# Attention scores of a head pair in a hybrid encoder kernel: zero-padded queries over all 128 rows against two heads on 64 rows each

## The chip, the cores and the metric

The kernel runs on one core of a Trainium2 chip. The metric is device time in microseconds (us) for one execution, as the median of several runs. The engines are named as in the profile: PE is the matrix engine and PEld its weight loads, DVE the vector engine, ACT the scalar engine, POOL the third elementwise engine, SP the queue that starts most transfers. A matmul here is two instructions: a load of the stationary operand (LDWEIGHTS, counted under PEld) and the MATMUL that streams the moving operand through it into PSUM. PSUM has eight banks of 128 partitions by 512 fp32 values.

## What is computed

The reference is an encoder of four layers on 512 tokens of width 1024: a convolution mixer, a neighbourhood attention, a retention, a convolution mixer, each followed by a gated feed-forward network. The change lies in the attention of layer 1 alone (16 heads of width 64, tokens on a grid of 8 rows by 64 columns):

```python
def nat_mixer(h, w_qkv, q_g, k_g, rpb, w_out):
    qkv = (h @ w_qkv).reshape(b, s, 3, NAT_HEADS, NAT_HEAD_DIM)
    q = rmsnorm(qkv[:, :, 0], q_g) * (NAT_HEAD_DIM ** -0.5)
    k = rmsnorm(qkv[:, :, 1], k_g)
    v = qkv[:, :, 2]
    ...
        sc = jnp.einsum('bhqd,bhrqwd->bhqrw', q_r, k_win).astype(jnp.float32)
        sc = sc + bias.transpose(0, 2, 1, 3)[None].astype(jnp.float32)
        p = jax.nn.softmax(sc.reshape(b, NAT_HEADS, GRID_W, kh * NAT_KW), axis=-1)
        ...
        return jnp.einsum('bhqrw,bhrqwd->bhqd', p, v_win)
    ...
    return out @ w_out
```

The scores `sc` are a product over the 64 values of one head.

## The kernel before

**Number format.** Every product is computed from fp32 data cut into a high and a low part of type fp32r; `mm3` (L158 to L161) issues three matmuls, high by high, high by low and low by high, into one PSUM region. `mm3s` (L164 to L166) is the same with the operands exchanged.

**The attention stage** (`nat`, L559) works on four groups `g` of four heads. `NORDER` says in which order its steps are written: `p0 a0 p1 a1 p2 w0 a2 p3 a3 w12 w3`. A step `p` (`proj`) projects q, k and v of a group: long runs of matmuls with 256 moving columns (L164 to L166). A step `a` (`att`) is the attention of a group, a step `w` (`wout`) the output projection of one or two groups, matmuls with 512 columns (L159 to L161, tiles oh and ol). The tile framework schedules the written program over the engines: it may move an instruction of one step between those of another, as its tiles and banks come free. So projections and attention stand mixed on PE, and each engine then executes its own list in order.

**Inside a step `a`** there are two pairs of heads (`pi` 0 and 1). `att_prep` (L635) transposes q and k of a pair on PE (L642), so that partitions 0 to 63 hold head 0 and 64 to 127 head 1, and copies them out of PSUM: k whole into kh and kl (L645, L646), q in four pieces into two tiles `qz[0]` and `qz[1]` (L650 on ACT, L651 on DVE). `qz[i]` has the queries of head `i` on that head's 64 partitions and zeros on the other 64; the zeros are written once at the head of the stage (L568 to L575, four DVE copies). `att_step` (L676) then handles one head and one half `pr` of the queries: it takes a PSUM bank S, writes the scores of two query blocks of 128 into it by `mm3`, with `qz[i]` as the stationary operand over all 128 rows of the array and 256 columns of kh or kl as the moving one (L683). The other head's keys meet the zeros. The softmax follows on DVE and ACT (L690 to L701), four transposes on PE (L703), the split into ph and pl (L706) and the product with v (L714: 12 matmuls with 64 stationary columns and 128 moving columns, shown as 128\*64). `att_pair` (L656) calls `att_step` for both heads, for each `pr`.

In all there are 4 groups, 2 pairs, 2 halves, 2 heads, 2 blocks and 3 products: 192 score matmuls.

Of the kernel before, what the change touches and what calls it, by code (L numbers as in the profile page):

```python
# [8 lines left out]
F32 = mybir.dt.float32  # L9
F32R = mybir.dt.float32r  # L10
I32 = mybir.dt.int32
AF = mybir.ActivationFunctionType
ALU = mybir.AluOpType
AX = mybir.AxisListType
MUL, ADD, SUB = ALU.mult, ALU.add, ALU.subtract
PSUM = bass.MemoryType.PSUM

P = 128
T = 512
# [51 lines left out]
def tile_trunk(  # L71
# [17 lines left out]
    def nm(s):  # L89
        uid[0] += 1  # L90
        return f"{s}{uid[0]}"
# [11 lines left out]
    def bank(which):  # L103
        return cur[which].tile([P, T], F32, tag="ps", name=nm("ps"))
# [25 lines left out]
    def pc(name, i=0, w=1):  # L130
        c = COLS[name] + i
        if c < 64:
            return png[:, c:c + w]
        return pt[:, c:c + w]
# [424 lines left out]
    def nat(after):  # L559
        PER = 4  # L560
        with ExitStack() as st:
# [3 lines left out]
            mask = np1.tile([P, 3, 256], F32, tag="mask", name=nm("mask"))  # L565
            nc.scalar.dma_start(mask, nmask.rearrange("p (v k) -> p v k", v=3))
            kstart = (0, 64, 192, 256)
            qzs = [[np1.tile([P, 2, T], F32R, tag=f"qz{n}{i}", name=nm("qz")) for i in range(2)]  # L568
                   for n in range(NQZ)]
            zz = np1.tile([P, 1], F32, tag="zz", name=nm("zz"))  # L570
            nc.vector.memset(zz, 0.0)
            for qz in qzs:
                for i in range(2):
                    zp = slice(64 - 64 * i, 128 - 64 * i)
                    nc.vector.tensor_copy(qz[i][zp], zz[zp].unsqueeze(2).broadcast_to([64, 2, T]))  # L575

            def part_proj(g, part):
                pss = [bank(psa), bank(psa)]
# [54 lines left out]
                return qk, va, vs  # L633

            def att_prep(g, pi, qk):  # L635
                qz = qzs[(2 * g + pi) % NQZ]
                kh = np2.tile([P, T], F32R, tag="kh", name=nm("kh"))
                kl = np2.tile([P, T], F32R, tag="kl", name=nm("kl"))
                for part in range(2):
                    ps = bank(psb)  # L640
                    for tb in range(4):
                        nc.tensor.transpose(ps[:, tb * P:(tb + 1) * P],  # L642
                                            qk[:, part, tb, pi * P:(pi + 1) * P], ident)
                    if part == 1:
                        nc.scalar.activation(kh, ps, AF.Copy, scale=pc("kg"))  # L645
                        nc.vector.scalar_tensor_tensor(kl, ps, pc("kg"), kh.bitcast(F32), MUL, SUB)  # L646
                    else:
                        for i in range(2):
                            r = slice(64 * i, 64 * i + 64)
                            nc.scalar.activation(qz[i][r, 0, :], ps[r], AF.Copy, scale=pc("qg")[r])  # L650
                            nc.vector.scalar_tensor_tensor(  # L651
                                qz[i][r, 1, :], ps[r], pc("qg")[r], qz[i][r, 0, :].bitcast(F32),
                                MUL, SUB)
                return qz, kh, kl

            def att_pair(g, pi, qz, kh, kl, va, vs):  # L656
                hi = np1.tile([P, T], F32R, tag="oh", name=nm("oh"), bufs=NO)
                lo = np1.tile([P, T], F32R, tag="ol", name=nm("ol"), bufs=NO)
                bms = []
                for i2 in range(2):  # L660
                    W = np2.tile([P, 384], F32, tag="W", name=nm("W"))
                    nc.sync.dma_start(W, wd[g * PER + pi * 2 + i2])
                    bm = np1.tile([P, 3, 256], F32, tag="bm", name=nm("bm"), bufs=NBM)
                    for vi, ws in enumerate((128, 64, 0)):
                        nc.gpsimd.tensor_tensor(bm[:, vi, :], W[:, ws:ws + 256],
                                                mask[:, vi, :], ADD)
                    bms.append(bm)
                for pr in range(2):
                    for i2 in range(2):
                        r = slice(64 * i2, 64 * i2 + 64)  # L670
                        c = slice(pr * 256, pr * 256 + 256)
                        op = att_step(g, pi, i2, pr, qz, kh, kl, bms[i2], va, vs)
                        state["att"] = split(op, hi[r, c], lo[r, c])
                return hi, lo

            def att_step(g, pi, i2, pr, qz, kh, kl, bm, va, vs):  # L676
                hh = pi * 2 + i2
                S = bank(psb)
                for i in range(2):
                    b = pr * 2 + i  # L680
                    ks = slice(kstart[b], kstart[b] + 256)
                    qs = slice(b * P, (b + 1) * P)
                    mm3(S[:, i * 256:(i + 1) * 256], qz[i2][:, 0, qs], qz[i2][:, 1, qs],  # L683
                        kh[:, ks], kl[:, ks], True, True)
                e = np1.tile([P, T], F32, tag="e", name=nm("e"), bufs=NE)
                mn, sx, rx = sm(2), sm(2), sm(2)
                for i in range(2):
                    vi = (0, 1, 1, 2)[pr * 2 + i]
                    ei = e[:, i * 256:(i + 1) * 256]
                    nc.vector.tensor_tensor_reduce(  # L690
                        ei, S[:, i * 256:(i + 1) * 256], bm[:, vi, :], -1.0, 3.0e38,
                        ADD, ALU.min, mn[:, i:i + 1])
                    nc.scalar.activation(ei, ei, AF.Exp, bias=mn[:, i:i + 1], scale=-1.0,
                                         accum_out=sx[:, i:i + 1])
                nc.vector.reciprocal(rx, sx)
                for i in range(2):
                    ei = e[:, i * 256:(i + 1) * 256]
                    if g == 3 and i == 1:
                        nc.scalar.activation(ei, ei, AF.Copy, scale=rx[:, i:i + 1])
                    else:  # L700
                        nc.vector.tensor_scalar(ei, ei, rx[:, i:i + 1], None, MUL)  # L701
                for i in range(4):
                    nc.tensor.transpose(S[:, i * P:(i + 1) * P], e[:, i * P:(i + 1) * P], ident)  # L703
                ph = np2.tile([P, T], F32R, tag="ph", name=nm("ph"))
                pl = np2.tile([P, T], F32R, tag="pl", name=nm("pl"))
                split(S, ph, pl)  # L706
                for i in range(2):
                    b = pr * 2 + i
                    vt, v0 = ((va, 0), (vs, 0), (vs, 1), (va, 2))[b]
                    oo = S[:64, i * P:(i + 1) * P]  # L710
                    for c in range(2):
                        hsl = slice(hh * HD, (hh + 1) * HD)
                        psl = slice((i * 2 + c) * P, (i * 2 + c + 1) * P)
                        mm3(oo, vt[:, v0 + c, 0, hsl], vt[:, v0 + c, 1, hsl],  # L714
                            ph[:, psl], pl[:, psl], c == 0, c == 1)
                return S[:64, :256]
# [472 lines left out]
```

## Time and profile before

| | us |
|---|---|
| median of 3 runs | 2584.52 (2584.17 to 2585.12) |
| profiled execution, whole | 2585.3 |
| its span, first to last instruction | 2583.5 |
| PE busy in the span | 2573.7 |
| attention stage, about | 584 to 836 of the span |

The span is what the profile's rows cover; the 1.8 us that the whole execution has beyond it lie outside. The stretches named below are in us from the span's start. A MATMUL's shown length includes the way through the array, so neighbours overlap; how fast matmuls follow each other is read from their starts. The granted clock of PE is 1.00 in every stretch shown, the higher of its two levels.

### The profile page before, as it was taken

How to read it: one execution, taken by the hardware profiler on the slowest of the kernel's cores; microseconds unless marked ns; L12 is line 12 of the kernel's file. 1: busy time of each engine (PE TensorE's matmuls, PEld its weight loads, DVE VectorE, ACT ScalarE, POOL GpSimd, SP SyncE). 2: the span in 40 equal slices, each digit the busy share in tenths (PEclk: the TensorE clock that was granted, in tenths of full speed). 3: DMA queues.
4: the chain of work that ended last, by engine and by line, in shares of the span. 5: the costliest groups of instructions: out<-in, count | busy, mean ns of one | idle time of the engine just before them, and what ended most of it. 6: DMA issues, size and time to landing. Idle time of an engine off the chain costs nothing.

```text
span 2583.5 us, 32274 instructions
## 1 busy us (share of the span) xinstructions
PE 2573.7 (100%) x12742; PEld 2138.2 (83%) x12742; DVE 1657.4 (64%) x2671; ACT 1047.0 (41%) x1437; POOL 229.7 (9%) x245
## 2 busy tenths in 40 slices
PE   9999999999999999999999999999999999999999
PEld 7988888889998888888888888888888888788888
DVE  7976777438877777634656566677743877677732
ACT  5454444335656444323332323444432445444421
POOL 0103000003421100000000000100000111100000
PEclk9999999999999999999999999999999999999999
DMA  6624222333332232333222221322233662222232
GB/s 227 223 82 153 97 91 96 90 100 111 96 91 70 98 98 90 94 97 110 74 84 72 84 80 58 99 97 92 95 90 99 212 192 79 90 90 98 89 109 80
DMA packets 78377, 269.86 MB, mean 104 GB/s; under 512 B 9825, under 2 KB 12769, under 8 KB 78225
## 3 DMA queue, kind: packets, MB, share of 16 engines
q1 hardware_dynamic: 73152, 254.49, 30.5%
q0 software_dynamic: 3776, 10.58, 1.5%
q10 hardware_dynamic: 1296, 2.72, 0.3%
q8 instruction: 100, 1.64, 0.3%
q14 instruction: 53, 0.43, 0.1%
HBM read 258.35 MB, written 5.63 MB: 102 GB/s over the span
## 4 chain that ended last, share of the span: by engine, by line
PE 98%; DVE 1%; ACT 0%; DMA 0%; issue 0%; SPq 0%; DVEq 0%
PE ps L161 28%; PE ps L160 27%; PE ps L159 27%; PE ps L460 3%; PE ps L165 3%; PE ps L166 3%; PE ps L164 3%; PE ps L463 1%; PE ps L327 1%; PE ps L332 1%; PE ps L328 1%; PE ps L703 1%; PE ps L518 0%; PE ps L642 0%; PE ps L932 0%; DVE qz L575 0%
## 5 line engine op out<-in xcount | busy, mean ns | idle before, releaser
L154 ACT CAST wh<-wr 128x1024 fp32r<-128x1024 f32 (+1 forms) x410 | 423.3, 1033 | 1075.8 <-PE ps L160 773.2
L161 PE MATMUL ps<-xh,wl 128*128 128x512 f32 x1856 | 738.3, 398 | 0.0
L160 PE MATMUL ps<-xl,wh 128*128 128x512 f32 x1856 | 733.9, 396 | 0.0
L159 PE MATMUL ps<-xh,wh 128*128 128x512 f32 x1856 | 730.4, 394 | 0.4 <-ACT xh L226 0.4
L155 DVE TENSOR_TENSOR wl<-wr,wh 128x1024 fp32r<-128x1024 f32 (+1 forms) x407 | 494.1, 1214 | 325.9 <-ACT wh L154 323.6
L160 PEld LDWEIGHTS ps<-xl,wh 128*128 128x128 f32 x1856 | 348.9, 188 | 88.2 <-DVE xl L229 0.5
L159 PEld LDWEIGHTS ps<-xh,wh 128*128 128x128 f32 x1856 | 349.0, 188 | 84.5 <-ACT xh L226 1.1
L161 PEld LDWEIGHTS ps<-xh,wl 128*128 128x128 f32 x1856 | 348.8, 188 | 80.5
L159 PE MATMUL ps<-hh,wh 128*128 128x512 f32 (+1 forms) x726 | 281.5, 388 | 0.5 <-DVE x L357 0.5
L161 PE MATMUL ps<-hh,wl 128*128 128x512 f32 (+1 forms) x726 | 281.5, 388 | 0.0
L160 PE MATMUL ps<-hl,wh 128*128 128x512 f32 (+1 forms) x726 | 281.5, 388 | 0.0
L293 DVE TENSOR_TENSOR t<-ps,rstd_bc 128x512 f32<-128x512 f32 x176 | 120.9, 690 | 159.5 <-PE ps L161 159.5
L247 POOL TENSOR_TENSOR sqacc<-t,sqacc 128x512 f32<-128x512 f32 x49 | 74.2, 1514 | 1258.5 <-ACT t L242 1258.0
L159 PEld LDWEIGHTS ps<-hh,wh 128*128 128x128 f32 x726 | 136.8, 188 | 30.7 <-DVE x L357 0.7
L160 PEld LDWEIGHTS ps<-hl,wh 128*128 128x128 f32 x726 | 136.8, 188 | 30.1
L161 PEld LDWEIGHTS ps<-hh,wl 128*128 128x128 f32 x726 | 136.8, 188 | 30.0
L165 PE MATMUL ps<-wl,xh 128*128 128x256 f32 (+1 forms) x512 | 159.2, 312 | 0.6 <-DVE wl L155 0.6
L166 PE MATMUL ps<-wh,xl 128*128 128x256 f32 (+1 forms) x512 | 159.1, 312 | 0.0
L164 PE MATMUL ps<-wh,xh 128*128 128x256 f32 (+1 forms) x512 | 158.5, 312 | 0.0
L296 ACT ACTIVATE t<-t,par 128x512 f32<-128x512 f32 x176 | 142.4, 813 | 6.0 <-DVE t L293 5.9
L300 DVE SCALAR_TENSOR_TENSOR t<-t,par,t 128x511 f32<-128x511 f32 x176 | 132.1, 751 | 5.5
L298 DVE SCALAR_TENSOR_TENSOR t<-t,par,t 128x511 f32<-128x511 f32 x176 | 130.8, 745 | 0.0
(251 smaller groups left out, 3439.2 us busy)
## 6 DMA issues: line engine op xcount, KB each, us to landing
wr<-in_f_up SPq DMA_DIRECT2D x176, 512.0 KB, 3.2
wraw<-in_cdw SPq DMA_DIRECT2D x56, 576.0 KB, 4.9
wr<-in_f_down SPq DMA_DIRECT2D x64, 448.0 KB, 3.3
wr<-in_f_down SPq DMA_DIRECT2D x32, 512.0 KB, 3.5
wr<-in_cw_in SPq DMA_DIRECT2D x30, 512.0 KB, 4.1
wr<-in_nat_qkv SPq DMA_DIRECT2D x24, 512.0 KB, 3.3
wr<-in_cw_out SPq DMA_DIRECT2D x16, 512.0 KB, 3.5
wr<-in_ret_qk SPq DMA_DIRECT2D x16, 512.0 KB, 3.2
```

The source lines that it names most:

```text
L154: nc.scalar.copy(hi[:, :n], raw[:, :n])
L155: eng.tensor_tensor(lo[:, :n], raw[:, :n], hi[:, :n].bitcast(F32), SUB)
L159: nc.tensor.matmul(o, wh, ah, start=first, stop=False)
L160: nc.tensor.matmul(o, wh, al, start=False, stop=False)
L161: nc.tensor.matmul(o, wl, ah, start=False, stop=last)
L164: nc.tensor.matmul(o, ah, wh, start=first, stop=False)
L165: nc.tensor.matmul(o, ah, wl, start=False, stop=False)
L166: nc.tensor.matmul(o, al, wh, start=False, stop=last)
L293: nc.vector.tensor_tensor(u, ps, rstd_bc, MUL)
L296: nc.scalar.activation(a, u, AF.Identity, bias=pc("fdb", l * 44 + c), scale=pt[:, w + 1:w + 2])
L298: nc.vector.scalar_tensor_tensor(a[:, 1:], u[:, :T - 1], pt[:, w:w + 1], a[:, 1:], MUL, ADD)
L300: nc.vector.scalar_tensor_tensor(a[:, :T - 1], u[:, 1:], pt[:, w + 2:w + 3], a[:, :T - 1], MUL, ADD)
```

## The change

The two zero-padded tiles of a pair become one tile `qz` that holds both heads, head 0 on partitions 0 to 63 and head 1 on 64 to 127. The zeros and the copies that wrote them go (L568 to L575). `att_prep` moves q out of PSUM with one ACT and one DVE instruction on 128 partitions in place of two and two on 64. The score matmuls leave `att_step` and become a function of their own, `scores`, that takes two PSUM banks, one for each head, and writes its 12 matmuls in turn: a matmul of head 0 with 64 stationary rows at rows 0 to 63 of the array, then one of head 1 at rows 64 to 127. Number, columns and result of the matmuls stay as they were; `att_step` gets its bank S filled.

```diff
-            qzs = [[np1.tile([P, 2, T], F32R, tag=f"qz{n}{i}", name=nm("qz")) for i in range(2)]
-                   for n in range(NQZ)]
-            zz = np1.tile([P, 1], F32, tag="zz", name=nm("zz"))
-            nc.vector.memset(zz, 0.0)
-            for qz in qzs:
-                for i in range(2):
-                    zp = slice(64 - 64 * i, 128 - 64 * i)
-                    nc.vector.tensor_copy(qz[i][zp], zz[zp].unsqueeze(2).broadcast_to([64, 2, T]))
...
-                qz = qzs[(2 * g + pi) % NQZ]
+                qz = np1.tile([P, 2, T], F32R, tag="qz", name=nm("qz"), bufs=NQZ)
...
-                        for i in range(2):
-                            r = slice(64 * i, 64 * i + 64)
-                            nc.scalar.activation(qz[i][r, 0, :], ps[r], AF.Copy, scale=pc("qg")[r])
-                            nc.vector.scalar_tensor_tensor(
-                                qz[i][r, 1, :], ps[r], pc("qg")[r], qz[i][r, 0, :].bitcast(F32),
-                                MUL, SUB)
+                        nc.scalar.activation(qz[:, 0], ps, AF.Copy, scale=pc("qg"))
+                        nc.vector.scalar_tensor_tensor(
+                            qz[:, 1], ps, pc("qg"), qz[:, 0].bitcast(F32), MUL, SUB)
...
                 for pr in range(2):
+                    Ss = scores(pr, qz, kh, kl)
                     for i2 in range(2):
...
-                        op = att_step(g, pi, i2, pr, qz, kh, kl, bms[i2], va, vs)
+                        op = att_step(g, pi, i2, pr, Ss[i2], bms[i2], va, vs)
...
-            def att_step(g, pi, i2, pr, qz, kh, kl, bm, va, vs):
-                hh = pi * 2 + i2
-                S = bank(psb)
+            def scores(pr, qz, kh, kl):
+                Ss = [bank(psb), bank(psb)]
                 for i in range(2):
                     b = pr * 2 + i
                     ks = slice(kstart[b], kstart[b] + 256)
                     qs = slice(b * P, (b + 1) * P)
-                    mm3(S[:, i * 256:(i + 1) * 256], qz[i2][:, 0, qs], qz[i2][:, 1, qs],
-                        kh[:, ks], kl[:, ks], True, True)
+                    for n, (qn, kt) in enumerate(((0, kh), (1, kh), (0, kl))):
+                        for i2, S in enumerate(Ss):
+                            r = slice(64 * i2, 64 * i2 + 64)
+                            nc.tensor.matmul(S[:, i * 256:(i + 1) * 256], qz[r, qn, qs], kt[r, ks],
+                                             start=n == 0, stop=n == 2)
+                return Ss
+
+            def att_step(g, pi, i2, pr, S, bm, va, vs):
+                hh = pi * 2 + i2
```

How the scheduler orders the result is seen in the built program. Numbers behind a tile's name tell its copies apart; "x2" is the same instruction twice.

On PE, in the first pair of group 0, second half of the queries, before (banks ps_5259 of head 0 and ps_5299 of head 1):

```order
L159 MATMUL ps_5259<-kh_5129,qz_4675 128x256
L160 MATMUL ps_5259<-kl_5130,qz_4675 128x256
L161 MATMUL ps_5259<-kh_5129,qz_4675 128x256
L159 MATMUL ps_5259<-kh_5129,qz_4675 128x256
L160 MATMUL ps_5259<-kl_5130,qz_4675 128x256
L161 MATMUL ps_5259<-kh_5129,qz_4675 128x256
L159 MATMUL ps_5299<-kh_5129,qz_4676 128x256
```

and the same place after (banks ps_5247 of head 0 and ps_5248 of head 1):

```order
L675 MATMUL ps_5247<-kh_5120,qz_5119 128x256
L675 MATMUL ps_5248<-kh_5120,qz_5119 128x256
L675 MATMUL ps_5247<-kh_5120,qz_5119 128x256
L675 MATMUL ps_5248<-kh_5120,qz_5119 128x256
L675 MATMUL ps_5247<-kl_5121,qz_5119 128x256
L675 MATMUL ps_5248<-kl_5121,qz_5119 128x256
```

The six matmuls of one head in a row became matmuls of the two heads in turn.

On PE, in the second pair of group 0, first half, before (bank ps_5393 is head 1; ps_5660 and ps_5259 belong to a projection and to the product with v):

```order
L164 MATMUL ps_5660<-wh_5670,xh_93 128x256
L159 MATMUL ps_5393<-kh_5147,qz_4678 128x256
L160 MATMUL ps_5393<-kl_5148,qz_4678 128x256
L161 MATMUL ps_5393<-kh_5147,qz_4678 128x256
L159 MATMUL ps_5393<-kh_5147,qz_4678 128x256
L160 MATMUL ps_5393<-kl_5148,qz_4678 128x256
L159 MATMUL ps_5259<-ph_5281,vs_5116 64x128
```

and the same place after (ps_5342 is head 1; ps_5648 belongs to a projection):

```order
L165 MATMUL ps_5648<-wl_5653,xh_89 128x256
L675 MATMUL ps_5342<-kh_5137,qz_5136 128x256 x2
L675 MATMUL ps_5342<-kl_5138,qz_5136 128x256
L675 MATMUL ps_5342<-kh_5137,qz_5136 128x256 x2
L675 MATMUL ps_5342<-kl_5138,qz_5136 128x256
L166 MATMUL ps_5648<-wh_5652,xl_97 128x256
```

Here the scheduler kept the matmuls of one head together, as the banks of the pair come free one after the other; those of head 0 (ps_5341) stand some 120 rows ahead. Counted over the stage, the 192 score matmuls stand in 25 unbroken runs before and in 25 after. In the runs of after, 43 neighbours can be paired as head 0 beside head 1 (86 matmuls, all of the first pair of a group); 106 matmuls stand behind one of their own head or alone.

On DVE, at the head of the stage, before:

```order
L229 SCALAR_TENSOR_TENSOR xl_102<-x_86,png,xh_94 128x8x64
L571 MEMSET zz_4679 128x1
L575 CAST qz_4675<-zz_4679 64x1024
L575 CAST qz_4676<-zz_4679 64x1024
L575 CAST qz_4677<-zz_4679 64x1024
L575 CAST qz_4678<-zz_4679 64x1024
L201 TENSOR_REDUCE sm_4753<-ps_4748 128x4
```

and after:

```order
L229 SCALAR_TENSOR_TENSOR xl_102<-x_86,png,xh_94 128x8x64
L201 TENSOR_REDUCE sm_4743<-ps_4738 128x4
L253 TENSOR_SCALAR sm_4745<-sm_4743 128x4
L174 TENSOR_SCALAR sm_4747<-sm_4745 128x4
L176 TENSOR_SCALAR sm_4749<-sm_4747 128x4
```

The statistics of the layer's norm (L201, L253 and on) follow at once on the last high-low split, where the four copies of zeros stood between them. Behind the attention stage the lists of all engines are the same before and after.

## Rows read from the trace of the kernel before

**Rows 1.** The page: span, busy time by engine, granted clock by slice, and the chain of work that ended last, by engine and by line.

```profile
span 2583.5 us, 32274 instructions
...
PE 2573.7 (100%) x12742; PEld 2138.2 (83%) x12742; DVE 1657.4 (64%) x2671; ACT 1047.0 (41%) x1437; POOL 229.7 (9%) x245
...
PEclk9999999999999999999999999999999999999999
...
PE 98%; DVE 1%; ACT 0%; DMA 0%; issue 0%; SPq 0%; DVEq 0%
PE ps L161 28%; PE ps L160 27%; PE ps L159 27%; PE ps L460 3%; PE ps L165 3%; PE ps L166 3%; PE ps L164 3%; PE ps L463 1%; PE ps L327 1%; PE ps L332 1%; PE ps L328 1%; PE ps L703 1%; PE ps L518 0%; PE ps L642 0%; PE ps L932 0%; DVE qz L575 0%
```

**Rows 2.** Busy time of each engine from 560 to 860 us, the attention stage with some of its neighbours.

```profile
core 0: us, PE busy (x) PEld busy (x) DVE busy (x) ACT busy (x) POOL busy (x), PEclk, DMA share, GB/s
560.00:860.00 300.00, 298.04 (x2324) 278.37 (x2323) 221.80 (x535) 161.19 (x342) 91.83 (x98) 1.00 0.31 95
```

**Rows 3.** For whom PE waited from 560 to 860 us: total, times, longest.

```profile
PE ps L159 <- DVE pl L170: 0.9, 2, 0.6
PE ps L165 <- DVE wl L155: 0.6, 1, 0.6
PE ps L159 <- ACT oh L169: 0.5, 1, 0.5
```

**Rows 4.** All instructions that write or read the tiles qz: durations of one in ns (least, median, most), first and last start in us.

```profile
L159 PEld LDWEIGHTS ps<-kh,qz x64: 187/188/193, 622.6 to 814.9; 128*128 128x128 f32 x64
L159 PE MATMUL ps<-kh,qz x64: 277/281/365, 622.7 to 815.0; 128*128 128x256 f32 x64
...
L650 ACT ACTIVATE qz<-ps,par x16: 682/684/692, 608.6 to 785.1; 64x512 fp32r<-64x512 f32 x16
L651 DVE SCALAR_TENSOR_TENSOR qz<-ps,par,qz x16: 734/750/759, 609.3 to 786.8; 64x512 fp32r<-64x512 f32 x16
L575 DVE CAST qz<-zz x4: 685/1131/1585, 584.7 to 588.1; 64x1024 fp32r<-64x1024 f32 x4
```

**Rows 5.** Timeline of PE and PEld, the first and the last instructions of an unbroken run of 28 score matmuls: start, length, engine, line. Between the two shown parts stand 23 more.

```profile
624.34 0.28 PE L160 MATMUL ps<-kl,qz 128*128 128x256 f32 x1
624.34 0.19 PEld L161 LDWEIGHTS ps<-kh,qz 128*128 128x128 f32 x1
624.46 0.28 PE L161 MATMUL ps<-kh,qz 128*128 128x256 f32 x1
624.46 0.19 PEld L159 LDWEIGHTS ps<-kh,qz 128*128 128x128 f32 x1
624.58 0.28 PE L159 MATMUL ps<-kh,qz 128*128 128x256 f32 x1
...
627.43 0.28 PE L160 MATMUL ps<-kl,qz 128*128 128x256 f32 x1
...
627.54 0.29 PE L161 MATMUL ps<-kh,qz 128*128 128x256 f32 x1
```

**Rows 6.** Timeline of PE where the product with v (128\*64, 128 moving columns) ends, a projection follows, and the next product begins.

```profile
636.05 0.22 PE L160 MATMUL ps<-pl,vs 128*64 128x128 f32 x1
636.11 0.22 PE L161 MATMUL ps<-ph,vs 128*64 128x128 f32 x1
636.17 0.33 PE L166 MATMUL ps<-wh,xl 128*128 128x256 f32 x1
636.34 0.28 PE L164 MATMUL ps<-wh,xh 128*128 128x256 f32 x1
636.45 0.28 PE L165 MATMUL ps<-wl,xh 128*128 128x256 f32 x1
636.57 0.28 PE L166 MATMUL ps<-wh,xl 128*128 128x256 f32 x1
636.69 0.22 PE L159 MATMUL ps<-ph,va 128*64 128x128 f32 x1
636.75 0.23 PE L160 MATMUL ps<-pl,va 128*64 128x128 f32 x1
```

**Rows 7.** Timeline of PEld at the first of these two changes.

```profile
636.05 0.14 PEld L161 LDWEIGHTS ps<-ph,vs 128*64 128x64 f32 x1
636.11 0.19 PEld L166 LDWEIGHTS ps<-wh,xl 128*128 128x128 f32 x1
636.22 0.19 PEld L164 LDWEIGHTS ps<-wh,xh 128*128 128x128 f32 x1
636.34 0.19 PEld L165 LDWEIGHTS ps<-wl,xh 128*128 128x128 f32 x1
```

**Rows 8.** Timeline of DVE at the head of the stage, with the ACT instruction that makes the high part of the weights of L155, and the PE matmul that waited behind them; in brackets the engine's idle time and what ended it.

```profile
583.20 1.33 DVE L229 SCALAR_TENSOR_TENSOR xl<-x,png,xh 128x512 fp32r<-128x512 f32 x1
584.48 0.06 DVE L571 MEMSET zz<- 128x1 f32 x1
584.66 4.57 DVE L575 CAST qz<-zz 64x1024 fp32r<-64x1024 f32 x4
589.16 0.67 DVE L201 TENSOR_REDUCE sm<-ps 128x4 f32<-128x512 f32 x1
...
591.40 1.06 ACT L154 CAST wh<-wr 128x1024 fp32r<-128x1024 f32 x1 [7.16 <-issue]
...
593.63 1.23 DVE L155 TENSOR_TENSOR wl<-wr,wh 128x1024 fp32r<-128x1024 f32 x1
...
594.92 0.39 PE L165 MATMUL ps<-wl,xh 128*128 128x256 f32 x1 [0.63 <-DVE wl L155]
```

**Rows 9.** Timeline of PE near the end of the last attention step, the three matmuls that waited.

```profile
819.73 0.28 PE L159 MATMUL ps<-ph,va 128*64 128x128 f32 x1 [0.27 <-DVE pl L170]
...
822.53 0.28 PE L159 MATMUL ps<-ph,vs 128*64 128x128 f32 x1 [0.60 <-DVE pl L170]
...
823.91 0.50 PE L159 MATMUL ps<-oh,wh 128*128 128x512 f32 x1 [0.45 <-ACT oh L169]
```

## The prediction

> **What bounds the kernel now.** First the page [rows 1]: PE is busy 2573.7 of 2583.5 us, the chain that ended last is 98% PE, and the granted clock is full in all 40 slices. So the time is the sum of the steps by which PE's matmuls follow each other, plus some 10 us of waits. Then the stage that the change touches [rows 2]: from 560 to 860 us PE is busy 298.04 of 300, with DVE at 221.80 and ACT at 161.19. Its waits there are 0.9, 0.6 and 0.5 us [rows 3]. A change in this stage pays only through PE's own steps and these 2 us; less work on DVE or ACT pays only where it ends one of those waits.
>
> Then the price of a score matmul. In an unbroken run of 28 [rows 5] the first starts at 624.34 and the last at 627.54: 3.20 us over 27 steps, 0.1185 us each, though each is shown 0.28 us long. The 192 of them cost 192 x 0.1185 = 22.8 us of PE, 0.9% of the kernel. The load of the next weights starts when the current matmul starts [rows 5]: one load is always under way beside one matmul. How long that load itself needs is seen where the matmul ahead is short [rows 6, 7]: behind a 128-column matmul the load of a projection starts at 636.11, and the following load, which starts with the projection's matmul, at 636.22. A load of 128 columns thus takes 0.11 us, nearly the step of a 256-column matmul. In the score runs load and matmul are balanced, and whatever saves on only one of them saves little.
>
> **The change, part by part.**
>
> *Two heads in turn.* The trace of before has no 64-row instruction, so its step is bounded from both sides. Best: the matmul of head 0 and that of head 1, on different rows, run beside each other and so do their loads; a pair then costs one step and not two. By the program's order only 43 such pairs exist (not 96: the second pair of every group keeps its heads apart), so 43 x 0.1185 = 5.1 us are saved. The other 106 matmuls stand behind one of the same rows and keep the step of 0.1185; a saving there is excluded, since a step goes with the moving columns (0.12 for 256, 0.06 for 128 [rows 6]) and those stay. Worst: nothing overlaps, 0 us. I take 5.1, since the two matmuls of a pair share neither operand rows nor a bank. That is the least certain term.
>
> *Changing the shape of the array.* The 25 runs give 25 entries and 25 exits between 128-row and 64-row matmuls. The nearest rows are the changes between 128\*128 and 128\*64 [rows 6]: into 128\*64 the step is 636.69 - 636.57 = 0.12, no extra; out of it the projection's matmul takes 0.17 (636.17 to 636.34) and not 0.12, 0.05 extra, which the exposed load explains. So the low end is 0. The high end would be an array that must be empty before the other shape may load: the matmul's shown end (0.28 behind its start) plus a shown load of 0.19 make a step of 0.47, 0.35 above 0.12, and 50 x 0.35 = 17.5 us. I take the row that is nearest in kind, a change of shape with the same engine state, at 0.05 once per run: 25 x 0.05 = 1.3 us.
>
> *The zeros.* The four copies hold DVE for 4.57 us from 584.66 on, and behind them are queued the layer's statistics and then the low part of a projection's weights (L155 at 593.63); PE waits 0.63 us for it at 594.92 [rows 8]. With the copies gone the statistics move ahead by 4.6 us. Next late is ACT's high part of the same weights, which ends at 591.40 + 1.06 = 592.46 [rows 8]: L155 can then start 593.63 - 592.46 = 1.17 us earlier, more than PE waits, so I count the whole 0.6 us as saved. Most of the 4.57 us was hidden by projection matmuls that PE had in hand.
>
> *Fewer, larger copies of q.* ACT loses 8 of 16 instructions of 0.684 us, 5.5 us; DVE 8 of 0.750, 6.0 us [rows 4]. The same 512 columns on twice the partitions are taken at the same time each, as the copy of k beside them is. PE waits for none of them [rows 3], so this counts 0; if PE's cover were gone it would be a gain, not a cost.
>
> *Two banks taken at once.* The first head's scores are complete only with the second's. If the pair overlaps, that is no later than before; if not, up to six steps (0.7 us) later. The work that covers it are the projection and output matmuls between the scores and the first product with v. Only at the end of the last step are they short, and there PE already waits 0.27, 0.60 and 0.45 us [rows 9]. The order of that place stays close to what it was; I count 0, between -0.9 (both waits for pl gone) and +1.4 (the 12 pairs that group 3 saves, 12 x 0.1185, given back as waiting).
>
> **Sum:** -5.1 + 1.3 - 0.6 = -4.4 us. Against the profiled execution, 2585.3 - 4.4 = 2580.9 us; its 1.8 us outside the span stay. The median of the runs is 0.8 us lower, so the forecast for the median is 2584.5 - 4.4 = **2580.1 us**. From this kernel's spread, about 0.2% (5.2 us) is what a measurement tells from no change; the forecast lies just inside it. Its own range goes from -6.6 (no cost of shapes, no waits for pl) to -2.9 (1.4 given back): 2577.9 to 2581.6.
>
> **The rivals.**
>
> *Rival 1: the two halves don't overlap (the change doesn't do what it says).* The matmuls may overlap but the loads come one after another, as every pair of loads in the trace does [rows 5, 7]. Then a pair costs 2 x 0.11 = 0.22 in place of 0.237, 43 x 0.017 = 0.7 us are saved, and the sum is -0.7 + 1.3 - 0.6 = 0: 2584.5 us. For it: loads and matmuls are balanced here, so halving only one brings nothing. Against: it is one set of rows that is loaded in all those loads.
>
> *Rival 2: slower, by emptying the array at each change of shape.* Place: the 50 borders of the runs. Price: the wait for the end of the matmul ahead, 0.28 - 0.12 = 0.16, and a load that can't be hidden, 0.11: 0.27 each, 13.5 us. With the pairs overlapping the sum is 13.5 - 5.1 - 0.6 = +7.8, 2592.3 us. It cancels the gain from 5.7 / 50 = 0.11 us a border, and makes the kernel slower by 0.2% from (5.7 + 5.2) / 50 = 0.22. Against it stand the borders of 128\*64 [rows 6], where nothing of the kind is seen; for it, that 128-row and 64-row matmuls write the same 128 partitions, which 128\*64, with half as many, does not test. The Trainium skill, TensorEngine Tiling (Array Packing), section Key Properties, states that changing the tiling mode drains the engine; the trace shows no drain at 128\*64 (0.00 and 0.05 us), and no run so far shows one at 64 rows.
>
> *Rival 3: slower, by loads that wait for the matmul on their own rows.* If 64-row loads are hidden only behind matmuls of the other half, the 106 unpaired matmuls show their load: 106 x 0.11 = 11.7 us, pairs gain nothing, and with -0.6 the sum is +11.1: 2595.6 us. Against: at 128 rows each load runs beside the matmul on its own rows [rows 5]. The Trainium skill, TensorE: Matmul & The Clock Gate, section Measured speedup vs the span model, says that weight loads overlap matmuls in flight only where the row group differs; the rows of this trace contradict it for 128 rows.
>
> **How the numbers follow.** Forecast (pairs overlap, borders cheap) 0.45; rival 1, 0.22; rival 2, 0.25, about half of it beyond +5.2 us; rival 3, 0.05; stalls elsewhere in the reordered stage 0.03. Faster by over 0.2%: two fifths of the forecast's case, 0.18. Slower: half of rival 2, rival 3 and most of the rest, 0.22. Within 0.2%: 0.60. The range reaches from the forecast's best case, 2577.9, to the price of rival 2, 2592.3; above it lie rival 3 and the dearest borders, some 0.14, below it 0.03.
>
> **What the changed kernel's profile would show.** Overlap: two 64-row matmuls, one on each half, start within a few hundredths of a us, and the next such pair 0.12 later; rival 1 shows equal steps near 0.11. Borders: the step into a run's first and out of its last matmul is 0.12 to 0.17; rival 2 shows 0.28 or more. Runs of six matmuls of one head take 0.12 a step; rival 3 shows 0.23. The zeros: PE's wait at L165 near 594 is gone and DVE's L201 starts about 4.6 us earlier. The waits at the end of the last step stay near 1.3 us. The prediction is wrong above all if a pair takes two steps, or if a border costs more than 0.11 us.

## The result and the profile after

The changed kernel takes 2588.44 us (median of 20 runs, 2587.70 to 2589.57) against 2584.40 us of the kernel before (20 runs, 2583.61 to 2585.77) on the same chip: a ratio of 1.0016 [1.0009, 1.0022]. It is **slower by 4.0 us** where 4.4 us less was forecast. The size is inside the 0.2% that the prediction took as its bound, and the time inside its range, but the sign is wrong. The profiled execution took 2589.3 us, its span 2587.5, so the 1.8 us outside the span did stay.

The page of the kernel after: span, busy time by engine, granted clock by slice, and the shares of the chain that ended last.

```profile
span 2587.5 us, 32248 instructions
...
PE 2576.0 (100%) x12742; PEld 2133.6 (82%) x12742; DVE 1647.7 (64%) x2658; ACT 1041.1 (40%) x1429; POOL 226.4 (9%) x245
...
PEclk9999999999999999999999999999999999999999
...
PE 99%; DVE 1%; DMA 0%; ACT 0%; issue 0%; SPq 0%; DVEq 0%
```

Against [rows 1] PE executes the same 12742 matmuls, at the same full clock, in 2.3 us more busy time. DVE and ACT lost 9.7 and 5.9 us, and none of that helps. From the first projection matmul of the stage to the last matmul on oh it took 252.29 us before (580.82 to 833.11) and takes 256.36 after (580.93 to 837.29). These 4.07 us are the whole loss: the cause lies inside the stage.

PE's waits from 555 to 865 us (total, times, longest):

```profile
PE ps L159 <- DVE pl L170: 1.7, 2, 1.0
PE ps L159 <- ACT oh L169: 0.5, 1, 0.5
```

Against [rows 3] the wait for wl at L165 is gone (-0.6) and the one for pl grew from 0.9 to 1.7 (+0.8). Such a wait is shown only from the shown end of the matmul ahead, some 0.16 us after its step is over. What a wait really costs is the time from the start of the matmul ahead to the start of the one that waited, less the usual step of the first: the wait for wl cost 0.80 us by this and not 0.63. Summed over all places in the stage where PE's rows show it idle, also those too short for the list, the waits cost 2.6 us before and 2.6 after, so they explain nothing of the 4 us. The rest must be in the steps. First the pairs, in a run of 26 score matmuls; timeline of PE (start, length, engine, line; "x4" is four rows in one, whose length is that of all):

```profile
622.32 0.28 PE L164 MATMUL ps<-wh,xh 128*128 128x256 f32 x1
622.52 0.39 PE L675 MATMUL ps<-kl,qz 64*128 64x256 f32 x2
622.74 0.40 PE L675 MATMUL ps<-kh,qz 64*128 64x256 f32 x4
622.98 0.28 PE L675 MATMUL ps<-kl,qz 64*128 64x256 f32 x2
623.10 0.40 PE L675 MATMUL ps<-kh,qz 64*128 64x256 f32 x4
...
624.41 0.28 PE L675 MATMUL ps<-kl,qz 64*128 64x256 f32 x1
624.62 0.38 PE L165 MATMUL ps<-wl,xh 128*128 128x256 f32 x1
624.84 0.28 PE L166 MATMUL ps<-wh,xl 128*128 128x256 f32 x1
```

Four matmuls (two on each half) take 622.74 to 622.98, two take 622.98 to 623.10: one step of 0.12 us for a pair, where [rows 5] show one for each matmul. So the overlap is there, loads included. But look at the borders. From the last projection matmul to the first pair it is 0.20 us and not 0.12, then 0.22 to the next pair; on the way out 0.21 and 0.22. Each border thus costs about 0.2 us, spread over two steps.

Where only one head's scores stand in a run nothing makes up for that. The smallest case is a run of a single matmul; timeline of PE, then of PEld:

```profile
672.64 0.28 PE L165 MATMUL ps<-wl,xh 128*128 128x256 f32 x1
672.75 0.28 PE L166 MATMUL ps<-wh,xl 128*128 128x256 f32 x1
672.97 0.38 PE L675 MATMUL ps<-kh,qz 64*128 64x256 f32 x1
673.28 0.39 PE L164 MATMUL ps<-wh,xh 128*128 128x256 f32 x1
673.50 0.28 PE L165 MATMUL ps<-wl,xh 128*128 128x256 f32 x1
```

```profile
672.64 0.19 PEld L166 LDWEIGHTS ps<-wh,xl 128*128 128x128 f32 x1
672.96 0.18 PEld L675 LDWEIGHTS ps<-kh,qz 64*128 64x128 f32 x1
673.28 0.19 PEld L164 LDWEIGHTS ps<-wh,xh 128*128 128x128 f32 x1
673.38 0.19 PEld L165 LDWEIGHTS ps<-wl,xh 128*128 128x128 f32 x1
```

The load of L166 starts at 672.64 with the matmul of L165 and hides beside it. The load of the score starts at 672.96, 0.21 us after the matmul ahead of it (672.75), whose 256 columns take 0.12: it is held for 0.09 us after the last column, and then nothing hides its own 0.11. The load of L164 at 673.28 is held in the same way. From 672.75 to 673.50 three steps take 0.75 us in place of 0.36; the run costs 0.39 beyond its matmul's own step.

The same for all 25 runs: of each I take the time from the start of the last other matmul ahead of it to the start of the second other one behind it, less the usual steps of those two (0.117 us for 256 columns, 0.234 for 512, 0.06 for 128 with 64 stationary columns, 0.108 for a transpose). The 192 score matmuls cost 22.86 us before by this and 26.85 after: **+3.99 us**, the whole loss but for 0.1. In the trace 46 pairs start within 0.03 us of each other, three more than stand as neighbours in the built order (half_rows_by_head below shows how that can be). With 46 pairs, 146 steps of 0.1185 make 17.30, so a run's two borders cost (26.85 - 17.30) / 25 = 0.38 us. The expectations below use 0.37, worked out with 43 pairs.

### The profile page after: what moved, and what is told of

Same layout as the page of the kernel before. It is cut to its first block, busy times and chain, and to the rows that moved or that the text cites. A ratio compares the mean times of both kernels' runs of the same rounds, so it can differ in the third digit from the quotient of the medians.

```text
span 2587.5 us, 32248 instructions
## 1 busy us (share of the span) xinstructions
PE 2576.0 (100%) x12742; PEld 2133.6 (82%) x12742; DVE 1647.7 (64%) x2658; ACT 1041.1 (40%) x1429; POOL 226.4 (9%) x245
## 4 chain that ended last, share of the span: by engine, by line
PE 99%; DVE 1%; DMA 0%; ACT 0%; issue 0%; SPq 0%; DVEq 0%
PE ps L161 27%; PE ps L159 27%; PE ps L160 27%; PE ps L460 3%; PE ps L165 3%; PE ps L166 3%; PE ps L164 3%; PE ps L463 1%; PE ps L675 1%; PE ps L327 1%; PE ps L328 1%; PE ps L332 1%; PE ps L699 1%; PE ps L518 0%; PE ps L928 0%; PE ps L634 0%
## 5 line engine op out<-in xcount | busy, mean ns | idle before, releaser
L161 PE MATMUL ps<-xh,wl 128*128 128x512 f32 x1856 | 737.7, 398 | 0.1
L160 PE MATMUL ps<-xl,wh 128*128 128x512 f32 x1856 | 733.2, 395 | 0.0
L159 PE MATMUL ps<-xh,wh 128*128 128x512 f32 x1856 | 729.9, 394 | 1.8 <-ACT wh L154 1.8
L155 DVE TENSOR_TENSOR wl<-wr,wh 128x1024 fp32r<-128x1024 f32 (+1 forms) x407 | 493.2, 1212 | 329.9 <-ACT wh L154 327.4
L160 PEld LDWEIGHTS ps<-xl,wh 128*128 128x128 f32 x1856 | 348.5, 188 | 87.1 <-DVE xl L229 0.5
L159 PEld LDWEIGHTS ps<-xh,wh 128*128 128x128 f32 x1856 | 348.6, 188 | 86.6 <-ACT wh L154 2.6
L161 PEld LDWEIGHTS ps<-xh,wl 128*128 128x128 f32 x1856 | 348.4, 188 | 81.0 <-DVE wl L155 0.5
L159 PE MATMUL ps<-hh,wh 128*128 128x512 f32 (+1 forms) x726 | 281.5, 388 | 0.5 <-DVE x L357 0.5
L161 PE MATMUL ps<-hh,wl 128*128 128x512 f32 (+1 forms) x726 | 281.5, 388 | 0.0
L160 PE MATMUL ps<-hl,wh 128*128 128x512 f32 (+1 forms) x726 | 281.4, 388 | 0.0
L159 PEld LDWEIGHTS ps<-hh,wh 128*128 128x128 f32 x726 | 136.8, 188 | 30.8 <-DVE x L357 0.7
L161 PEld LDWEIGHTS ps<-hh,wl 128*128 128x128 f32 x726 | 136.8, 188 | 30.2
L160 PEld LDWEIGHTS ps<-hl,wh 128*128 128x128 f32 x726 | 136.8, 188 | 29.8
L165 PE MATMUL ps<-wl,xh 128*128 128x256 f32 (+1 forms) x512 | 159.9, 314 | 0.0
L166 PE MATMUL ps<-wh,xl 128*128 128x256 f32 (+1 forms) x512 | 159.4, 312 | 0.0
L164 PE MATMUL ps<-wh,xh 128*128 128x256 f32 (+1 forms) x512 | 158.6, 313 | 0.0
```

The lines of the kernel that those rows point to most:

```text
L155: eng.tensor_tensor(lo[:, :n], raw[:, :n], hi[:, :n].bitcast(F32), SUB)
L159: nc.tensor.matmul(o, wh, ah, start=first, stop=False)
L160: nc.tensor.matmul(o, wh, al, start=False, stop=False)
L161: nc.tensor.matmul(o, wl, ah, start=False, stop=last)
L164: nc.tensor.matmul(o, ah, wh, start=first, stop=False)
L165: nc.tensor.matmul(o, ah, wl, start=False, stop=False)
```

## The experiments

Each row is one kernel: its median; the ratio to the kernel before on the same chip with its interval; unbroken runs of score matmuls in the built order (of 64-row ones alone in the two first_pairs kernels) and pairs that start within 0.03 us of each other in the trace; what the score matmuls cost on PE (worked out as above); length of the attention stage; PE's waits in it as the profile shows them; and what these waits cost, counted from start to start as above.

| kernel | us | ratio | runs, pairs | scores us | stage us | waits shown us | waits cost us |
|---|---|---|---|---|---|---|---|
| before | 2584.40 | 1 | 25, 0 | 22.86 | 252.29 | 2.0 | 2.6 |
| after | 2588.44 | 1.0016 [1.0009, 1.0022] | 25, 46 | 26.85 | 256.36 | 2.2 | 2.6 |
| full_rows_in_turn | 2585.58 | 1.0005 [0.9996, 1.0014] | 30, 0 | 22.99 | 253.02 | 2.3 | 3.3 |
| half_rows_by_head | 2590.67 | 1.0025 [1.0015, 1.0035] | 28, 44 | 28.26 | 258.20 | 2.0 | 2.7 |
| turns_kept | 2583.28 | 0.9997 [0.9988, 1.0006] | 18, 90 | 18.90 | 251.21 | 3.3 | 4.8 |
| first_pairs_early | 2587.87 | 1.0014 [1.0005, 1.0023] | 6, 47 | 19.73 | 255.35 | 5.2 | 8.4 |
| first_pairs_only | 2583.68 | 0.9999 [0.9990, 1.0008] | 8, 45 | 20.77 | 251.79 | 2.9 | 4.0 |
| turns_w0_late | 2579.33 | 0.9981 [0.9972, 0.9990] | 18, 91 | 18.81 | 247.17 | 1.1 | 1.4 |
| before_w0_late | 2582.01 | 0.9992 [0.9983, 1.0001] | 29, 0 | 22.82 | 249.93 | 0.7 | 0.9 |

In every row the change in scores and the change in what waits cost give the change in the stage's length within 0.7 us.

### Is it the rows, or the order and the two banks?

**full_rows_in_turn** keeps the changed order and both banks at once, but with the zero-padded queries over all 128 rows:

```diff
-    nc.tensor.matmul(S[...], qz[r, qn, qs], kt[r, ks], ...)
+    nc.tensor.matmul(S[...], qz[i2][:, qn, qs], kt[:, ks], ...)
```

> The changed kernel with the zero-padded queries and 128-row matmuls of before: same two banks at once, same two heads in turn, no 64-row instruction. Theory (the changed kernel saves 43 x 0.1185 = 5.1 us by overlapping pairs and pays about 0.37 us for each of its 25 runs, 9.2 us, at the changes of shape): without 64-row matmuls both go, 192 x 0.1185 = 22.8 us of score steps as before, so within 1 us of the kernel before, 2584.4. Rival (the new order and the two banks at once cost the time, not the shape): it stays at the changed kernel's 2588.4.

Measured: 1.3 us above before, a little more than the 1 us expected, with an interval that holds no change; 0.7 of it are waits. The scores cost 22.99 us, 0.1 more than before, though they stand in 30 runs. A border between 128-row matmuls costs nothing. The order and the two banks are not the cause.

**half_rows_by_head** takes the 64 rows alone: each head takes its own bank as before, all six matmuls of a head in one call.

```diff
+    S = bank(psb)
+    r = slice(64 * i2, 64 * i2 + 64)
...
+        mm3(S[...], qz[r, 0, qs], qz[r, 1, qs], kh[r, ks], kl[r, ks], True, True)
```

> 64-row matmuls as in the changed kernel, but head by head inside the step of one head, one bank at a time, as written before. The built order has 28 unbroken runs and only 19 places where the two heads can be paired. Theory: 28 x 0.37 = 10.4 paid, 19 x 0.1185 = 2.3 saved, 0.6 for the zeros: +7.5 us, about 2592, slower than the changed kernel. Rival (order and banks cost the time): as the kernel before or 0.6 below it, 2584.

Measured: +6.35 us. The scores cost 28.26 us, 5.40 more than before, so the rival falls. But the trace shows 44 pairs and not 19. Timeline of PE at the head of a run of 28, where the built order has five matmuls of head 0 (L160, L161, L159, L160, L161) and then five of head 1 with the same lines:

```profile
622.01 0.38 PE L160 MATMUL ps<-kl,qz 64*128 64x256 f32 x1
622.23 0.28 PE L161 MATMUL ps<-kh,qz 64*128 64x256 f32 x1
622.24 0.39 PE L160 MATMUL ps<-kl,qz 64*128 64x256 f32 x1
622.35 0.28 PE L159 MATMUL ps<-kh,qz 64*128 64x256 f32 x1
622.47 0.28 PE L161 MATMUL ps<-kh,qz 64*128 64x256 f32 x1
622.47 0.28 PE L160 MATMUL ps<-kl,qz 64*128 64x256 f32 x1
```

The L160 at 622.24 is not head 0's second one, which stands behind its L159 (622.35). It is head 1's first, and it starts beside head 0's second matmul, ahead of three matmuls that stand before it in the built order. The 28 matmuls start within 1.99 us, 17 steps in place of 27. So the heads need not alternate in the program: inside a run the two halves went on side by side, each in its own order.

With 44 pairs a run's borders cost (28.26 - 148 x 0.1185) / 28 = 0.38 us, as in the changed kernel. The scores cost 1.41 us more than there for three more runs (1.1) and two fewer pairs (0.2). That the time came near the expectation was luck in part: the expectation had 25 pairs too few, 3.0 us, and no new waits.

### The price of a border by itself

Into the feed-forward network of the kernel before, 168 times, goes one more matmul of 256 columns ahead of a projection whose first matmul overwrites what it wrote. The result of the extra matmul is used nowhere. Three kernels differ in its shape alone: 64 rows by 128 columns of the array, 128 by 128, and 128 by 64.

```diff
+    nc.tensor.matmul(ps[:, :256], wh[:64, :P], xhi[0][:64, :256], ...)   # one_more_half
+    nc.tensor.matmul(ps[:, :256], wh[:, :P], xhi[0][:, :256], ...)       # one_more_full
+    nc.tensor.matmul(ps[:64, :256], wh[:, :64], xhi[0][:, :256], ...)    # one_more_narrow
```

> The price of a border by itself, away from the attention: the kernel before with one more matmul in front of each of 168 accumulations of the feed-forward up projections (42 in each layer), 64 rows by 128 columns, 256 moving columns, into the same bank, overwritten by the first real matmul; the output does not change. Theory: each costs its step and two borders of 0.2, 0.118 + 0.37 to 0.40, 168 x 0.50 = 84 us: about 2668. In the trace the load of the added matmul starts about 0.1 after the matmul ahead has streamed, and so does the next load. Rival (a 64-row matmul costs its step alone): 168 x 0.118 = 20 us, 2604.

> As the run with one more 64-row matmul, but 128 rows by 128 columns, no change of shape: the price of the added matmul alone. All theories: 168 x 0.118 = 20 us, about 2604. The difference to the 64-row one is the price of two borders.

> As the run with one more 64-row matmul, but 128 rows by 64 stationary columns: another shape (128*64) with all rows. Theory (the border belongs to the change in rows; none was seen at 128*64 in the attention): its step alone, 168 x 0.118 = 20 us, about 2604, and its load starts with the matmul ahead. Rival (every change of shape empties the array): as the 64-row one, about 2673.

Measured: one_more_half 2673.38 us, ratio 1.0344 [1.0325, 1.0363], +89.1 us or 0.530 each. one_more_full 2605.51, 1.0083 [1.0064, 1.0101], +21.3 or 0.127 each, little more than a matmul's step of 0.1185. one_more_narrow 2605.63, 1.0083 [1.0065, 1.0101]. So two borders of 64 rows cost (2673.38 - 2605.51) / 168 = 0.404 us, **0.202 us each**, and those of 128\*64 nothing. The runs of scores give nearly the same for two borders: 0.38 us in the changed kernel, half_rows_by_head and both kernels with kept turns, about 0.42 in the two kernels with first pairs.

Of one_more_half, all instructions of the added line and the idle time ahead of them, then timelines of PE and PEld at one of them:

```profile
L280 PEld LDWEIGHTS ps<-xh,wh x168: 182/183/184, 221.1 to 2537.1; 64*128 64x128 f32 x168
...
  issue: 59.8, 168
```

```profile
860.05 0.40 PE L328 MATMUL ps<-xh,wh 128*128 128x512 f32 x1
860.28 0.39 PE L329 MATMUL ps<-xh,wl 128*128 128x512 f32 x1
860.60 0.38 PE L280 MATMUL ps<-xh,wh 64*128 64x256 f32 x1
860.91 0.49 PE L159 MATMUL ps<-xh,wh 128*128 128x512 f32 x1
861.25 0.40 PE L160 MATMUL ps<-xl,wh 128*128 128x512 f32 x1
```

```profile
860.60 0.18 PEld L280 LDWEIGHTS ps<-xh,wh 64*128 64x128 f32 x1 [0.36 <-issue]
860.91 0.19 PEld L159 LDWEIGHTS ps<-xh,wh 128*128 128x128 f32 x1
861.02 0.19 PEld L160 LDWEIGHTS ps<-xl,wh 128*128 128x128 f32 x1
```

The matmul at 860.28 has 512 columns, 0.23 us by the step ahead of it; the 64-row load comes 0.32 after its start, again 0.09 after its last column. In all 168 places the load engine stands idle, 59.8 us in sum, and the profile names no releaser ("issue"): nothing that a semaphore shows holds it. one_more_narrow has no such idle time; its loads:

```profile
L280 PEld LDWEIGHTS ps<-xh,wh x168: 134/134/137, 220.9 to 2469.6; 128*64 128x64 f32 x168
```

### Fewer borders, more pairs

**turns_kept** ties each score matmul behind the one before it, so that the scheduler can't break up the 12 of a pair of heads, and writes head 1 and the product that needs kl first:

```diff
-    for n, (qn, kt) in enumerate(((0, kh), (1, kh), (0, kl))):
-        for i2, S in enumerate(Ss):
+    for n, (qn, kt) in enumerate(((0, kl), (1, kh), (0, kh))):
+        for i2, S in reversed(list(enumerate(Ss))):
...
+            with tc.issue_after(mm.ins) if mm is not None else ExitStack():
```

> The changed kernel with each of the 12 score matmuls of a call queued behind the one before it, starting with head 1 (whose bank comes last) and with the product of kl: the scheduler can no longer take the heads apart. The built order has 18 runs in place of 25 and 90 pairs in place of 43. Theory: 102 steps x 0.1185 = 12.1, and 18 x 0.37 = 6.7, 18.8 us of scores against 22.8 before; with 0.6 for the zeros -4.6 us: about 2580, faster than both kernels. Rival (order and banks cost the time): at or above the changed kernel, 2588 or more. A third possibility is that the scores of the second pair now wait for two banks and PE runs out of other work: then PE shows waits of several tenths of a us at the ends of the steps, and the gain shrinks.

Measured: 2583.28 us, 1.0 below before with an interval that holds no change. The steps came as worked out: 18.90 us for the scores with 90 pairs in 18 runs, 4.0 less than before. Only a quarter of it arrives. PE's waits in the stage:

```profile
PE ps L701 <- DVE e L699: 2.2, 3, 1.1
PE ps L159 <- DVE pl L170: 0.6, 1, 0.6
PE ps L159 <- ACT oh L169: 0.5, 1, 0.5
```

The transposes now wait for the softmax (L701 is the line of L703 in the code before): the chain from scores to the product with v has its own length, and where PE has no other matmuls left it waits for it. Counted from start to start the waits cost 4.8 us. The expectation left 1.8 (2.6 less the 0.80 for wl), so waits account for 3.0 of the 3.6 us missing from the expected 4.6; the rest lies in steps beside the transposes and elsewhere. Waits of several tenths of a us were the third possibility of the expectation; that the wait for two banks makes them is not shown.

**first_pairs_early** and **first_pairs_only** give 64 rows to the first pair of each group alone, and write all its 24 matmuls in one row; the second pair keeps the zero-padded 128 rows. first_pairs_early writes them even ahead of the second pair's transposes:

```diff
-    pre = [att_prep(g, pi, qk) for pi in range(2)]
+    pre = [att_prep(g, 0, qk)]
+    state["pairs"] = [scores(pr, *pre[0]) for pr in range(2)]
+    pre.append(att_prep(g, 1, qk))
```

> 64-row matmuls in turn for the first pair of each group alone, its 24 score matmuls of both query halves chained into one another and written ahead of the second pair's transposes, so that its four banks are free at once; the second pair keeps the zero-padded 128-row matmuls of before, head by head, with one set of zeros (two copies). The built order has 6 runs of 64-row matmuls (24, 24, 14, 7, 3 and 24) and 47 pairs. Theory: 47 x 0.1185 = 5.6 saved, 6 x 0.40 = 2.4 paid, 0.6 saved at the zeros: -3.8 us, about 2580.6, as long as PE's waits at the ends of the steps stay at 2 us. Rival for the shortfall of the run with the kept turns (that the chain itself or the 64-row matmuls delay the softmax, not the wait for two banks): the waits for e and pl stay near 3 us here too and the time is 2582 or more.

> The same, but with the transposes of both pairs written first, as in both kernels so far: banks come free in two steps, the built order has 8 runs (13, 11, 13, 11, 8, 5, 11, 24) and 43 pairs. Theory: 43 x 0.1185 = 5.1 saved, 8 x 0.40 = 3.2 paid, 0.6 saved at the zeros: -2.5 us, about 2582; the second pair's order is that of before, so the waits stay near 2 us.

Measured: 2587.87 and 2583.68 us. In both the scores cost less by about what was expected (19.73 and 20.77 us). first_pairs_early is still slower than before by 3.6 us, a miss of 7. Its waits:

```profile
PE ps L724 <- DVE e L722: 3.5, 6, 0.6
PE ps L159 <- DVE pl L170: 1.2, 3, 0.5
PE ps L159 <- ACT oh L169: 0.5, 1, 0.5
```

Counted from start to start its 16 waits, most of them for e, cost 8.4 us, 5.8 more than before. That takes back the 3.1 us that the scores save, and what is left over is most of the 3.1 us by which its stage is longer. first_pairs_only, which lacks mainly the later writing of the second pair's transposes, pays 4.0 us for waits and is 4.2 us faster. That points to the second pair's softmax, which starts later in first_pairs_early; no run isolates it. The rival's sign (waits near 3 us, 2582 or more) is there in both runs, so they don't clear the chain or the 64-row matmuls of delaying the softmax.

### Work for PE while the softmax runs

If the lost gain of turns_kept went into waits for want of other matmuls, then a step `w0` (the output projection of group 0) moved behind `p3` should cover the last attention steps. **turns_w0_late** is turns_kept with that, **before_w0_late** the kernel before with that alone:

```diff
-NORDER = "p0 a0 p1 a1 p2 w0 a2 p3 a3 w12 w3".split()
+NORDER = "p0 a0 p1 a1 p2 a2 p3 w0 a3 w12 w3".split()
```

> The run with the kept turns, and the output projection of group 0 moved in the written order from behind p2 to behind p3, so that its 48 matmuls of 512 columns (11 us) can fill PE while the softmax of the last group runs. 18 runs, 91 pairs. Theory (the score steps are saved, 4 us, and the zeros 0.8, but the softmax chain of the last group then leaves PE without work, which gave most of it back as waits for e and pl): with work moved there the waits in the last step shrink from 2.6 to under 1 us, and the time is about 2580. Rival (the waits come from the two banks at once, in whatever step): the waits move with the order, and the time stays near 2583.

> Control for the run beside it: the kernel before with the same move of group 0's output projection and nothing else. Its PE waits in the stage are 2.0 us in all, of which 1.3 at the end of the last step, so the move can save 1.3 us at most: 2583 to 2584.5 by either theory. What the other run has beyond this belongs to the 64-row scores.

Measured: turns_w0_late 2579.33 us, 4.8 below before and 9.1 below the changed kernel. It beats both, and its interval lies below 1. PE in the stretch of [rows 2], and its waits:

```profile
560.00:860.00 300.00, 298.94 (x2348) 273.36 (x2347) 218.63 (x530) 157.46 (x338) 92.76 (x98) 1.00 0.30 96
```

```profile
PE ps L701 <- DVE e L699: 0.6, 1, 0.6
PE ps L159 <- ACT oh L169: 0.5, 1, 0.5
```

Shown waits fell from 3.3 to 1.1 us (from 4.8 to 1.4 counted from start to start), with the chain of the kept turns in place, and PE is busy 298.94 of 300. before_w0_late gains 2.1 us by the move alone, where at most 1.3 was expected, though its interval just holds no change. The bound of 1.3 was read from the shown waits; counted from start to start they fell by 1.8 us. So of the 4.8 us the move has 2.1, and the 64 rows kept together have 2582.01 - 2579.33 = 2.7 (between two medians of the same chip). Their score steps save 22.82 - 18.81 = 4.0; 0.5 of the missing 1.3 are waits (1.4 against 0.9), 0.8 is not placed.

## Why the prediction was wrong

**The step that failed** is the term "Changing the shape of the array". It was put at 0.05 us once per run, 1.3 us in all, by the row of 128\*64 as the nearest in kind. A run's two borders cost 0.38 us in this kernel and 0.404 in one_more_half less one_more_full: 25 x 0.38 = 9.5 us. The term is inside its bounds (0 to 17.5) and seven times too small. With 9.5 for 1.3 the sum of the prediction is -5.1 + 9.5 - 0.6 = +3.8. With the other terms as measured below it is -5.5 (46 pairs) + 9.5 - 0.8 (zeros) + 0.8 (waits for pl) = +4.0, and 4.0 was measured. The 0.38 is read from the changed kernel itself; the price from the feed-forward network, 0.404, would make the borders 10.1 us and the sum +4.6. The row of 128\*64 was the wrong neighbour: one_more_narrow shows that shape to cost nothing at 168 clean places. The prediction named the reason why it might not carry over (128\*64 writes half the partitions), and took it all the same.

**Rival 2** had the mechanism right: a load held until the array has streamed the matmul ahead, and then exposed. Its price of 0.27 us a border was too high; 0.20 was measured. It read the hold from the matmul's shown end, 0.28 behind its start, and the load comes 0.21 behind it. What is measured lies above its break-even of 0.11, and so the kernel became slower; a quarter of the chances had stood on this rival. The Trainium skill, TensorEngine Tiling (Array Packing), section Key Properties, says that switching the tiling mode drains the engine: for 64 rows against 128 rows the runs agree, at 0.202 us a border; for 128\*64 they show no drain.

**Two heads in turn** was right in its price: a pair takes 0.12 us, and 46 of them save 5.5. Its count, 43, took neighbours in the built order for the only possible pairs, which half_rows_by_head refutes (44 pairs, 19 neighbours); here it cost 0.4 us, since most other runs hold one head alone. With the price of a pair, rival 1 falls (it had 0.22). **Rival 3** falls as well. Six matmuls of one head in a run, timeline of PE:

```profile
638.87 0.28 PE L165 MATMUL ps<-wl,xh 128*128 128x256 f32 x1
639.08 0.51 PE L675 MATMUL ps<-kh,qz 64*128 64x256 f32 x2
639.43 0.28 PE L675 MATMUL ps<-kl,qz 64*128 64x256 f32 x1
639.55 0.40 PE L675 MATMUL ps<-kh,qz 64*128 64x256 f32 x2
639.78 0.28 PE L675 MATMUL ps<-kl,qz 64*128 64x256 f32 x1
639.99 0.39 PE L166 MATMUL ps<-wh,xl 128*128 128x256 f32 x1
```

From 639.43 on a step takes 0.12: loads on the same 64 rows hide beside the matmul ahead. The 0.35 for the first two is the entry's exposed load, 0.11, and two steps. So the sentence of the Trainium skill that rival 3 names (TensorE: Matmul & The Clock Gate; it stands in the section The mechanism) does not hold for six matmuls on one half either.

**The zeros** were put at 0.6 us, the shown wait; the wait that went had cost 0.8, counted from start to start. The way was in part another than foretold. Timeline of DVE at the head of the stage:

```profile
588.85 0.69 DVE L201 TENSOR_REDUCE sm<-ps 128x4 f32<-128x512 f32 x1 [4.27 <-PE ps L199]
...
592.59 1.23 DVE L155 TENSOR_TENSOR wl<-wr,wh 128x1024 fp32r<-128x1024 f32 x1 [0.17 <-ACT wh L154]
```

L201 starts 0.31 us earlier than in [rows 8], not 4.6: it waits 4.27 us for PE's transposes (L199), which the zeros had hidden. L155 starts 1.04 earlier, behind ACT's wh, close to the 1.17 predicted, and PE's wait is gone.

**Fewer, larger copies of q**: ACT's takes 0.69 us and DVE's 0.74, as before each, and nobody waited for the others; 0 was right. **Two banks taken at once** was put at 0 between -0.9 and +1.4, and the waits for pl measured +0.8. Taking the banks together is not what made it, since full_rows_in_turn does that and waits 0.9 for pl as before; half_rows_by_head, with 64 rows and single banks, waits 1.5. The borders in the last step, where PE has little else, are the likelier cause; no run isolates it. A slip in the sum: the weak end of its own range should be -4.4 + 1.4 = -3.0, not -2.9; nothing hangs on it.

## What to carry to other kernels

Two 64-row matmuls on the two halves of the array run in the time of one, but the way into such a run and out of it costs 0.40 us together, what 0.40 / 0.1185 = 3.4 pairs of 256 columns save: it pays only if one unbroken run holds more pairs than that. So count the runs in the built order and keep the 64-row matmuls of both halves together in few long ones. Within a run the halves need not alternate: the trace shows which matmuls started beside each other. When a price is not in the trace, a neighbour that differs in what may matter is no measurement, and one added instruction at many clean places measures it. On an engine that is nearly always busy, time saved ahead of a chain of softmax and transposes comes back as waiting unless other matmuls are left to fill it. What such a wait costs is read from start to start, since the shown one begins only at the shown end of the matmul ahead.

## What had not been expected of the hardware

A border between 128-row and 64-row matmuls costs 0.202 us in either direction on average (0.09 of held load, 0.11 of exposed load), at the full granted clock, while one between 128\*128 and 128\*64 costs none (2605.63 against 2605.51 us for 168 matmuls). Within a run of 64 rows nothing is held: loads of both halves run beside each other, and each load beside the matmul ahead on its own half, at 0.12 us a step. And PE did not keep to the order of the program between the halves: in half_rows_by_head a matmul of head 1 started ahead of three of head 0 that stand before it, and 44 pairs ran side by side where the built order has 19 neighbours.
